# Copies for sums in DRAM, spread behind the weight loads, and six plain chunks at the head of the FFN

## The chip, the cores and the metric

The kernel runs on one NeuronCore of a Trainium2 chip. The metric is the device time of one launch in microseconds: 1307.48 us for the kernel before (median of two runs, 1306.55 and 1308.41). A core has five engines that run side by side, each with its own in-order queue: TensorE (PE, matmuls into PSUM), VectorE (DVE), ScalarE (ACT), GpSimd (POOL), and SyncE (SP), which here only issues DMAs. Sixteen DMA engines move the data for all of them.

## The reference

Two layers of a decoder trunk over 512 tokens of width 1024, in float32. Each layer normalises its input, multiplies it with one wide input weight, runs four groups of heads on parts of the result (attention with a forget gate "f", gated linear attention "g", latent attention "m", and a state-space scan "s"), multiplies their joint output with `w_out`, adds that to the residual, and runs a gated FFN:

```python
for l in range(DEPTH):
    h = rmsnorm(x, norm1[l])
    (fq, fk, fv, ff, gq, ...) = split_cols(h @ w_in[l], IN_SPLITS)
    ...
    x = x + mix @ w_out[l]
    h2 = rmsnorm(x, norm2[l])
    x = x + (silu(h2 @ w_gate[l]) * (h2 @ w_up[l])) @ w_down[l]
return rmsnorm(x, final_norm)
```

The FFN is 2816 wide, 22 chunks of 128 columns.

## The kernel before

All activations stay in SBUF, transposed (features on partitions, 512 tokens along the row). Every weight is cut on the host into units of 128 x 1024 floats (512 KB), in the order in which they are used. Float32 precision is reached with three matmuls per product: weight and activation are each split into a high and a low part, and `prod` (L425) multiplies high by high, low by high and high by low. So each unit is loaded by SP (L314, tile "wr", two buffers), split by ScalarE (the high part "wh", L331) and VectorE (the low part "wl", L332, three buffers each) and then read by 24 matmuls.

A layer takes 34 units ahead of its FFN: two for the first columns, "sm" for the small ones, eight for the convolution and gate columns ("ft"), then "fk", "fq", "fv", "fk", "fq", "mckv", "mcq", "gq", "gk", "gv" and the rest, and eight for `w_out`. Between these products the four groups run as generators, a step at a time. POOL takes part in them: it fills "fkb" and "fqb" (L1227, L1228), multiplies "ce" (L752) and "ssm_mix" (L774) for the scan "s", whose products on TensorE are called "y" (L766, L770), and "gmn" (L797), and clears "gat" (L881) for "g".

The FFN runs in three parts of 8, 8 and 6 chunks of hidden columns; each part ends with eight units of `w_down` ("d"). The first `PLAIN` chunks of the first part are plain: a unit of `w_gate` ("g") and one of `w_up` ("u"), 24 matmuls of 512 columns each. The others go in pairs of chunks: the two chunks and the two halves of the tokens and features form 2 x 2 blocks, multiplied with seven products of half size in place of eight (`pair_products`, L489). A pair has 14 such products, each 12 matmuls of 256 columns. It needs sums of blocks of the activation, which the class `Halves` makes on ScalarE and VectorE, one `chunk(k)` (L467) for each of four feature chunks k, behind plain chunk k. And it needs sums of quadrants of the weights. Those are made in two ways. A pair unit (a gate or an up weight) takes three units of the weight array. `pair_load` (L370) brings two tiles of it to SBUF, "px" and "pz", half of each from the weights and half from a tensor "sum" in DRAM, and "pv"; `pairs` adds two more sums on VectorE (L416, L417), and `pair_part` splits each into high and low ("pX", "pY", "pZ", "pV").

The tensors "sum" are made by `background` (L388), a step of which is called for every unit that is split. SP copies a unit of the weights within DRAM to a new "sum" (L399), and later POOL issues a DMA that adds another unit to it (L395). That POOL instruction waits until its copy has landed. The list `todo` holds the pair units of both layers, 36; a step is taken from the sixth call on, at each call while more than 18 are left, then at every second.

Outside the few stretches under a manual schedule, a scheduler sets the order of the instructions on each engine; it is free to move an instruction that depends on nothing, as a copy within DRAM, ahead of others that come earlier in the code. `tc.issue_after(ins)` is a bound on it: the instructions of the block on the engine of `ins` stand behind `ins` in its queue. It adds no wait on the chip.

Of the kernel before, what the change touches and what calls it, by code (L numbers as in the profile page):

```python
# [52 lines left out]
ACT_SET = "natural_log_exp_and_others"  # L53
HID_PARTS = ((0, 8), (8, 16), (16, 22))

PLAIN = 4
HALF = KC // 2
PAIR_AHEAD = 3
EARLY = 3
# [12 lines left out]
def _weights(I, depth=2):  # L72
# [3 lines left out]
    def add(*ws):  # L76
        u = np.concatenate([_unit(w) for w in ws], 1)
        shapes.append((u.shape[1] // ws[0].shape[1], ws[0].shape[1]))
        units.append(np.pad(u, ((0, 0), (0, 1024 - u.shape[1]))))

    for l in range(depth):
# [25 lines left out]
        for j0, j1 in HID_PARTS:  # L107
            for j in range(j0, min(j1, PLAIN)):
                add(I["w_gate"][l][:, j * P:j * P + P])
                add(I["w_up"][l][:, j * P:j * P + P])  # L110

            paired[len(units)] = (j1 - max(j0, PLAIN)) // 2, not j0
            for j in range(max(j0, PLAIN), j1, 2):

# [35 lines left out]
def trunk(tc, I, out, shapes, paired, depth=2):  # L150
    nc = tc.nc
    PE, V, S, G = nc.tensor, nc.vector, nc.scalar, nc.gpsimd

    def blk(i, n=P):
        return slice(i * n, (i + 1) * n)

    from contextlib import ExitStack
    with ExitStack() as es:
# [14 lines left out]
        def ps_proj(name):  # L173
            return pj.tile([P, T], F32, tag="pj", name=name)

        def ps_mix(name):
            return pm.tile([P, T], F32, tag="pm", name=name)
# [13 lines left out]
        def tmp(tag, name, cols=T, dt=F32, parts=P):  # L191
            return mp.tile([parts, cols], dt, tag=tag, bufs=RINGS[tag], name=name)
# [107 lines left out]
        class Weights:  # L300
# [7 lines left out]
            def load(self, parts=1):  # L308
                i, (nk, ncol) = self.n, shapes[self.n]
                self.n += 1  # L310
                raw = wp.tile([P, 1024], F32, tag="wr", bufs=RAWS, name=f"wr{i}")
                self.loaded.append((raw, i, nk, ncol))
                for c in (blk(j, nk * ncol // parts) for j in range(parts)):
                    nc.sync.dma_start(raw[:, c], I["weights"][i][:, c])  # L314
                    yield

            def split(self, pieces=1):

                if not self.loaded:
                    list(self.load())  # L320

                    if self.n + EARLY in paired and not paired[self.n + EARLY][1]:
                        n, self.n = self.n, self.n + EARLY
                        self.early = self.pair_load(True)
                        self.early_n, self.n = self.n, n
                self.background()
                raw, i, nk, ncol = self.loaded.pop(0)
                n = nk * ncol
                h, lo = (wp.tile([P, 1024], F32R, tag=f"w{c}", bufs=PARTS, name=f"w{c}{i}") for c in "hl")
                for c in (blk(j, n // pieces) for j in range(pieces)):  # L330
                    S.copy(h[:, c], raw[:, c])  # L331
                    V.tensor_tensor(lo[:, c], raw[:, c], h.bitcast(F32)[:, c], op=ALU.subtract)  # L332
                    yield h, lo
                self.ready.append(tuple(t[:, :n].rearrange("p (k c) -> p k c", k=nk) for t in (h, lo)))

            def prefetch(self, n):
# [51 lines left out]
            def background(self):  # L388

                self.turn += 1  # L390
                if self.turn < 6 or self.turn % 2 and len(self.todo) <= 18:
                    return
                if len(self.copied) > (3 if self.todo else 0):
                    i, t = self.copied.pop(0)
                    nc.gpsimd.dma_start(t, I["weights"][i + 2], accum_op=ALU.add, max_dma_last_dim=4096)  # L395
                if self.todo:
                    i = self.todo.pop(0)
                    t = self.sums[i] = dp.tile([P, 1024], F32, name=f"sum{i}")
                    nc.sync.dma_start(t, I["weights"][i + 1])  # L399
                    self.copied.append((i, t))  # L400
# [26 lines left out]
        def prod(ps, w, act, c0=0, ks=None, t=slice(0, T), nk=None, between=lambda: None):  # L427

            wh, wl = w
            n = len(act) if ks is None else nk or KC  # L430
            for k in range(n) if ks is None else ks:
                ah, al = (a[:, t] for a in act[k])
                PE.matmul(ps, lhsT=wh[:, k, c0:c0 + P], rhs=ah, start=k == 0, stop=False)  # L433
                between()
                PE.matmul(ps, lhsT=wl[:, k, c0:c0 + P], rhs=ah, start=False, stop=False)  # L435
                between()
                last = PE.matmul(ps, lhsT=wh[:, k, c0:c0 + P], rhs=al, start=False, stop=k == n - 1)  # L437
            return last
# [692 lines left out]
        for l in range(depth):  # L1131
# [14 lines left out]
            for j in range(10):  # L1146
# [11 lines left out]
                else:  # L1158
                    c = tmp("f", f"cv{l}_{j}")
# [165 lines left out]
            for j0, j1 in HID_PARTS:  # L1325
                us = []
                for j in range(j0, min(j1, PLAIN)):
                    pg, pu = ps_proj(f"g{l}_{j}"), ps_mix(f"u{l}_{j}")
                    if r is None:
                        r = norm2.first_two(pg, pu, KC - 2, with_col=False)  # L1330
                    else:
                        prod(pg, W.get(), act)
                    t, s = tmp("f", f"ft{l}_{j}"), tmp("f", f"fs{l}_{j}")
                    V.tensor_tensor(t, pg, r, op=ALU.mult)
                    silu = S.activation(s, t, AF.Silu)
                    G.tensor_tensor(s, s, r, op=ALU.mult)
                    if j:
                        prod(pu, W.get(), act)
                    V.tensor_tensor(t, pu, s, op=ALU.mult)
                    uh, ul = tmp("a", f"uh{l}_{j}", dt=F32R), tmp("b", f"ul{l}_{j}", dt=F32R)  # L1340
                    S.copy(uh, t)
                    V.tensor_tensor(ul, t, uh.bitcast(F32), op=ALU.subtract)
                    us.append((uh, ul))
                    if j == 0:
                        quads = Halves(l, 16 + l * 8, r)
                    quads.chunk(j)
                lo, hi = slice(0, 256), slice(256, 512)
                for j in range(max(j0, PLAIN), j1, 2):
                    s1, s2, end = pair_products(f"g{l}_{j}", quads.act)
                    S.activation(s1, s1, AF.Silu)  # L1350
                    S.activation(s2[:, hi], s2[:, hi], AF.Silu, scale=-1.0)
                    silu = S.activation(s2[:, lo], end, AF.Silu, scale=-1.0)
                    t1, t2, end = pair_products(f"u{l}_{j}", quads.act)
                    V.tensor_tensor(t1, t1, s1, op=ALU.mult)
                    V.scalar_tensor_tensor(t2[:, hi], t2[:, hi], -1.0, s2[:, hi], op0=ALU.mult, op1=ALU.mult)
                    V.scalar_tensor_tensor(t2[:, lo], end, -1.0, s2[:, lo], op0=ALU.mult, op1=ALU.mult)
                    for i, t in enumerate((t1, t2)):
                        uh, ul = tmp("a", f"uh{l}_{j + i}", dt=F32R), tmp("b", f"ul{l}_{j + i}", dt=F32R)
                        S.copy(uh, t)
                        V.tensor_tensor(ul, t, uh.bitcast(F32), op=ALU.subtract)  # L1360
                        us.append((uh, ul))
                if j1 == HC:
                    with tc.issue_after(silu.ins):
                        S.preload_act_table_set(ACT_SET)
                if j1 == HC and last_layer:
                    last_part(us)
                    continue
                for m in range(KC):
                    ps = ps_proj(f"d{l}_{j0}_{m}")
                    prod(ps, W.get(), us)  # L1370
                    V.tensor_tensor(xT[m], xT[m], ps, op=ALU.add)  # L1371
                    if j1 == HC:
                        norm.chunk(m)
                        norm.square(m)
# [25 lines left out]
```

## Time and profile before

| | us |
|---|---|
| runs shown: median of 2 (lowest, highest) | 1307.48 (1306.55, 1308.41) |
| profiled execution, its time | 1306.41 |
| its span, first to last instruction | 1304.7 |
| TensorE busy (7702 matmuls) | 1220.3 (94%) |
| VectorE busy | 862.6 (66%) |
| ScalarE busy | 652.5 (50%) |
| POOL busy | 132.9 (10%) |
| DRAM copies and accumulates | 36 and 36, 512 KB each |

The chain that ended last is 67% TensorE, 9% DMA, 9% issue and 8% VectorE. Busy shares are means over stages that differ: a share of 94% says nothing of a stage in which TensorE stands still. Matmuls overlap, so that one lasts 389 ns in the records while the next starts after some 230; durations of a row of matmuls are read from start to start. The granted clock of TensorE is 1.00 or 0.50 at a time (2.4 or 1.2 GHz), and a figure between is a mean over a stretch.

### The profile page before, as it was taken

What the parts mean: (1) busy time and instruction counts of PE and PEld (TensorE: products, weight loads), DVE (VectorE), ACT (ScalarE), POOL (GpSimd) and SP (SyncE); (2) the same over time, 40 slices, a digit from 0 to 9 for tenths busy, and PEclk for the clock granted to TensorE, in tenths of its full rate; (3) what the DMA queues carried; (4) which work ended last, traced back from release to release, by engine and by line L of the source; (5) the groups of instructions that cost most, each with busy time, mean ns of one, the idle gap of its engine ahead of it and who ended that gap; (6) DMA issues with size and microseconds to landing.
All of it is one profiled execution on the core that took longest, in us unless ns stands there. A gap on an engine that the chain in (4) does not pass through costs nothing.

```text
span 1304.7 us, 19729 instructions
## 1 busy us (share of the span) xinstructions
PE 1220.3 (94%) x7702; PEld 1058.7 (81%) x7702; DVE 862.6 (66%) x1476; ACT 652.5 (50%) x1126; POOL 132.9 (10%) x151
## 2 busy tenths in 40 slices
PE   8887089999979999999999999999997999999997
PEld 7766068777869899989988887877887989988986
DVE  6654158976887367637755767985888537854764
ACT  5334167574655145515553468857555425533542
POOL 1221243010010000000030012210010000000001
PEclk9989589999989999999999999999998999999999
DMA  9999971122245234423233221121234424341322
GB/s 279 314 298 305 257 155 58 49 66 64 78 149 170 88 110 133 134 73 112 63 105 97 94 84 51 42 69 61 66 114 163 131 84 140 114 142 61 114 62 77
DMA packets 54814, 157.42 MB, mean 121 GB/s; under 512 B 6976, under 2 KB 7136, under 8 KB 54144
## 3 DMA queue, kind: packets, MB, share of 16 engines
q1 hardware_dynamic: 48528, 136.60, 31.6%
q0 software_dynamic: 5760, 18.96, 7.7%
q8 instruction: 60, 0.98, 0.3%
q10 hardware_dynamic: 432, 0.60, 0.2%
q14 instruction: 34, 0.28, 0.1%
HBM read 153.97 MB, written 39.85 MB: 149 GB/s over the span
## 4 chain that ended last, share of the span: by engine, by line
PE 67%; DMA 9%; issue 9%; DVE 8%; ACT 4%; POOL 2%; SPq 0%; DVEq 0%; POOLq 0%; ACTq 0%
PE d L437 5%; PE d L435 5%; PE d L433 5%; DMA sum<-in_weights_dram 4%; DMA wr<-in_weights_dram 4%; PE ft L433 2%; PE ft L437 1%; PE ft L435 1%; DVE wl L332 1%; PE oa L433 1%; PE dl L433 1%; PE dl L437 1%; PE dl L435 1%; PE oa L437 1%; PE sm L918 1%
## 5 line engine op out<-in xcount | busy, mean ns | idle before, releaser
L331 ACT CAST wh<-wr 128x1024 fp32r<-128x1024 f32 (+2 forms) x134 | 134.4, 1004 | 255.9 <-PE d L437 87.8
L332 DVE TENSOR_TENSOR wl<-wr,wh 128x1024 fp32r<-128x1024 f32 (+2 forms) x134 | 156.5, 1168 | 88.0 <-ACT wh L331 87.6
L433 PE MATMUL d<-uh,wh 128*128 128x512 f32 x304 | 118.3, 389 | 0.0
L435 PE MATMUL d<-uh,wl 128*128 128x512 f32 x304 | 118.3, 389 | 0.0
L437 PE MATMUL d<-ul,wh 128*128 128x512 f32 x304 | 118.3, 389 | 0.0
L1371 DVE TENSOR_TENSOR xT<-xT,d 128x512 f32<-128x512 f32 x40 | 27.5, 688 | 98.7 <-PE d L437 98.7
L437 PEld LDWEIGHTS d<-ul,wh 128*128 128x128 f32 x304 | 57.1, 188 | 11.8
L435 PEld LDWEIGHTS d<-uh,wl 128*128 128x128 f32 x304 | 57.1, 188 | 11.7
L433 PEld LDWEIGHTS d<-uh,wh 128*128 128x128 f32 x304 | 57.1, 188 | 11.7
L395 POOL DMA_DIRECT2D sum<-in_weights_dram x36 | 30.4, 868 | 114.1 <-DMA sum<-in_weights_dram 114.1
L586 POOL TENSOR_TENSOR n_1acc<-n_1acc,n_1q 128x512 f32<-128x512 f32 x6 | 9.7, 1614 | 299.1 <-ACT n_1q L585 296.8
L433 PE MATMUL ft<-n_0h,wh 128*128 128x512 f32 x80 | 33.9, 424 | 6.4 <-ACT fo L1166 3.5
L1007 POOL TENSOR_TENSOR nfacc<-nfacc,nfq 128x512 f32<-128x512 f32 x5 | 8.0, 1610 | 297.4 <-ACT nfq L1003 297.4
L435 PE MATMUL ft<-n_0h,wl 128*128 128x512 f32 x80 | 33.0, 412 | 0.1
L437 PE MATMUL ft<-n_0h,wh 128*128 128x512 f32 x80 | 32.9, 411 | 0.0
L770 PE MATMUL y<-ce,st 128*64 128x128 f32 x48 | 6.6, 312 | 26.7 <-POOL ce L752 26.7
L435 PE MATMUL ft<-n_1h,wl 128*128 128x512 f32 x80 | 31.3, 391 | 0.0
L433 PE MATMUL ft<-n_1h,wh 128*128 128x512 f32 x80 | 31.3, 391 | 0.0
L437 PE MATMUL ft<-n_1h,wh 128*128 128x512 f32 x80 | 31.2, 390 | 0.0
L1166 ACT ACTIVATE fo<-fa 128x512 f32<-128x512 f32 x20 | 12.4, 629 | 31.5 <-DVE fa L1164 28.3
L1164 DVE SCALAR_TENSOR_TENSOR fa<-cv,pcv,fa 128x511 f32<-128x511 f32 (+2 forms) x36 | 26.9, 748 | 0.7
L770 PEld LDWEIGHTS y<-ce,st 128*64 128x64 f32 x48 | 4.6, 158 | 27.5 <-POOL ce L752 27.5
(2618 smaller groups left out, 4237.1 us busy)
## 6 DMA issues: line engine op xcount, KB each, us to landing
wr<-in_weights_dram SPq DMA_DIRECT2D x112, 512.0 KB, 3.5
sum<-in_weights_dram SPq DMA_DIRECT2D x36, 512.0 KB, 14.8
sum<-in_weights_dram POOLq DMA_DIRECT2D x36, 512.0 KB, 24.3
px<-in_weights_dram SPq DMA_DIRECT2D x36, 256.0 KB, 4.3
px<-sum SPq DMA_DIRECT2D x36, 256.0 KB, 4.7
pz<-sum SPq DMA_DIRECT2D x36, 256.0 KB, 2.8
pz<-in_weights_dram SPq DMA_DIRECT2D x36, 256.0 KB, 3.2
pv<-in_weights_dram SPq DMA_DIRECT2D x36, 256.0 KB, 3.5
```

The source lines that it names most:

```text
L331: S.copy(h[:, c], raw[:, c])
L332: V.tensor_tensor(lo[:, c], raw[:, c], h.bitcast(F32)[:, c], op=ALU.subtract)
L395: nc.gpsimd.dma_start(t, I["weights"][i + 2], accum_op=ALU.add, max_dma_last_dim=4096)
L433: PE.matmul(ps, lhsT=wh[:, k, c0:c0 + P], rhs=ah, start=k == 0, stop=False)
L435: PE.matmul(ps, lhsT=wl[:, k, c0:c0 + P], rhs=ah, start=False, stop=False)
L437: last = PE.matmul(ps, lhsT=wh[:, k, c0:c0 + P], rhs=al, start=False, stop=k == n - 1)
L586: (adds or (V if k == KC - 1 else G)).tensor_tensor(self.acc, self.acc, sq, op=ALU.add)
L770: PE.matmul(y[blk(hh, 64), blk(b)], lhsT=sv[b - 1][:, blk(2 * g + hh, 64)], rhs=ces[hh][:, blk(b - 1)], start=False, stop=True)
L918: PE.matmul(ps[:, :n], lhsT=q[:d, blk(qb)], rhs=k[:d, :n], start=i == 0, stop=i == len(terms[h]) - 1)
L1164: V.scalar_tensor_tensor(a[:, n:], c[:, :T - n], wc(3 - n), a[:, n:], op0=ALU.mult, op1=ALU.add)
L1166: silu = S.activation(o, a, AF.Silu)
L1371: V.tensor_tensor(xT[m], xT[m], ps, op=ALU.add)
```

## The change

`background` is called behind the split of a unit instead of ahead of it, inside `tc.issue_after` of the last weight load that was traced. It acts at every second call from the sixth on, whatever is left. An accumulate follows when more than one copy is outstanding, where it was more than three. `PLAIN` is 6 instead of 4, so that the first part of each FFN has six plain chunks and one pair (four plain and two pairs before), and `todo` holds 32 pair units. `Halves.chunk` still runs four times, behind the first four plain chunks.

```diff
-PLAIN = 4
+PLAIN = 6
 HALF = KC // 2
...
             def load(self, parts=1):
...
-                    nc.sync.dma_start(raw[:, c], I["weights"][i][:, c])
+                    self.last_load = nc.sync.dma_start(raw[:, c], I["weights"][i][:, c])
                     yield
...
             def split(self, pieces=1):
...
-                self.background()
                 raw, i, nk, ncol = self.loaded.pop(0)
...
                     yield h, lo
+                with tc.issue_after(self.last_load.ins):
+                    self.background()
...
             def background(self):
                 self.turn += 1
-                if self.turn < 6 or self.turn % 2 and len(self.todo) <= 18:
+                if self.turn < 6 or self.turn % 2:
                     return
-                if len(self.copied) > (3 if self.todo else 0):
+                if len(self.copied) > (1 if self.todo else 0):
...
-                    quads.chunk(j)
+                    if j < HALF:
+                        quads.chunk(j)
```

The order of the instructions moves at three places. The first is SP's queue after the load of the input; "wr" is the load of a weight unit, "sum" a copy within DRAM. Before:

```order
L198 DMA xT_92<-in_x_dram 128x512
L314 DMA wr_241<-in_weights_dram 128x1024
L314 DMA wr_311<-in_weights_dram 128x1024
L399 DMA sum_401<-in_weights_dram 16x8192
L399 DMA sum_452<-in_weights_dram 16x8192
L314 DMA wr_317<-in_weights_dram 128x1024
L399 DMA sum_506<-in_weights_dram 16x8192
L399 DMA sum_548<-in_weights_dram 16x8192
L314 DMA wr_399<-in_weights_dram 128x1024
```

Now:

```order
L198 DMA xT_92<-in_x_dram 128x512
L314 DMA wr_241<-in_weights_dram 128x1024
L314 DMA wr_311<-in_weights_dram 128x1024
L314 DMA wr_317<-in_weights_dram 128x1024
L314 DMA wr_399<-in_weights_dram 128x1024
L400 DMA sum_405<-in_weights_dram 16x8192
L314 DMA wr_450<-in_weights_dram 128x1024
L314 DMA wr_502<-in_weights_dram 128x1024
L400 DMA sum_508<-in_weights_dram 16x8192
```

Before, all 36 copies of the program stand ahead of the 21st load of a weight; now a copy stands behind every second load, 21 of 32 ahead of the first pair of layer 0 and the other 11 among the loads of that layer's `w_down`.

The second place is POOL's queue around the scan of layer 0. Before:

```order
L1228 DMA fqb_0_887<-jrr_441 2x512
L1228 DMA fqb_1_896<-jrr_441 2x512
L395 DMA sum_3772<-in_weights_dram 128x1024
L395 DMA sum_3837<-in_weights_dram 128x1024
L395 DMA sum_3913<-in_weights_dram 128x1024
L752 TENSOR_TENSOR ce_0_1003<-ce_0_1003,fo_8_714 128x384
L395 DMA sum_3980<-in_weights_dram 128x1024
L395 DMA sum_5052<-in_weights_dram 128x1024
```

Now:

```order
L1229 DMA fqb_1_883<-jrr_441 2x512
L753 TENSOR_TENSOR ce_0_987<-ce_0_987,fo_8_707 128x384
L396 DMA sum_1069<-in_weights_dram 128x1024
L753 TENSOR_TENSOR ce_1_1051<-ce_1_1051,fo_8_707 128x384
L1228 MEMSET fkb_2_1097 4x512
L1229 DMA fkb_2_1097<-jrr_441 2x512
L396 DMA sum_1267<-in_weights_dram 128x1024
L1228 MEMSET fkb_3_1106 4x512
L775 TENSOR_TENSOR ssm_0mix<-ssm_0mix,fo_2_433 128x512
```

Before, 31 accumulates stand ahead of the first "ce" and 35 ahead of the second; now 6 and 7.

The third place is VectorE's queue at the last chunk of `Halves` in layer 0 ("xn", "bn", "bd" and the low parts "bsl", "b21l", "bd1l", "bd3l"). Before:

```order
L416 TENSOR_TENSOR px_3198<-px_3198 128x512
L1339 TENSOR_TENSOR ft_3_3241<-u_3_3197,fs_3_3242 128x512
L417 TENSOR_TENSOR px_3198<-px_3198,pz_3199 128x512
L472 SCALAR_TENSOR_TENSOR xn_3_3285<-xT_88,pcv,n_0r 128x512
L1342 TENSOR_TENSOR ul_3_3282<-ft_3_3241,uh_3_3281 128x512
L369 TENSOR_TENSOR pY42l<-px_3198,pY42h 128x1024
L369 TENSOR_TENSOR pZ42l<-pz_3199,pZ42h 128x1024
L472 SCALAR_TENSOR_TENSOR xn_7_3287<-xT_92,pcv,n_0r 128x512
```

Now:

```order
L331 TENSOR_TENSOR wl_3211<-wr_3208,wh_3210 128x1024
L1340 TENSOR_TENSOR ft_3_3203<-u_3_3172,fs_3_3204 128x512
L331 TENSOR_TENSOR wl_3275<-wr_3272,wh_3274 128x1024
L1343 TENSOR_TENSOR ul_3_3243<-ft_3_3203,uh_3_3242 128x512
L473 SCALAR_TENSOR_TENSOR xn_3_3246<-xT_88,pcv,n_0r 128x512
L473 SCALAR_TENSOR_TENSOR xn_7_3248<-xT_92,pcv,n_0r 128x512
```

The sums and splits of the first pair's weights stood between the operations of the last chunk; now the splits of two more plain units stand there, and the pair's come behind the chunk.

## Rows read from the trace of the kernel before

**Rows 1.** The profile's 40 slices: busy tenths, granted clock and DMA share in tenths.
```profile
PE   8887089999979999999999999999997999999997
...
PEclk9989589999989999999999999999998999999999
DMA  9999971122245234423233221121234424341322
```
**Rows 2.** Windows "sm" to "mckv", both layers: length, busy (records) by engine, PEclk, DMA, GB/s.
```profile
19.60:179.10 159.50, 105.01 (x512) 86.55 (x511) 72.76 (x139) 52.05 (x86) 40.90 (x55) 0.83 1.04 283
693.60:787.30 93.70, 93.41 (x506) 78.82 (x506) 65.84 (x122) 49.81 (x81) 11.76 (x18) 1.00 0.29 91
```
**Rows 3.** Waits of PE, 0 to 180 us: us in total, times, longest.
```profile
PE y L770 <- POOL ce L752: 26.7, 2, 22.6
PE y L766 <- DVE sw L759: 11.8, 1, 11.8
```
**Rows 4.** Waits of POOL and ACT, 0 to 185 us.
```profile
POOL sum L395 <- DMA sum<-in_weights_dram: 114.1, 31, 16.2
ACT wh L331 <- DMA wr<-in_weights_dram: 61.5, 14, 8.6
```
**Rows 5.** DMA, 0 to 200 us: queues (packets, MB, engines' share); weight loads, median landing.
```profile
q0 software_dynamic: 5504, 18.93, 50.1%
q1 hardware_dynamic: 5953, 33.24, 44.2%
...
wr<-in_weights_dram SPq DMA_DIRECT2D x22, 512.0 KB, 10.7
```
**Rows 6.** Line 399, the copies: ns of issue, first and last start; landing.
```profile
L399 SPq DMA_DIRECT2D sum<-in_weights_dram x36: 488/587/867, 12.9 to 122.0; - x36
...
DMA to landing us min/median/max: 6.0/14.8/21.0
```
**Rows 7.** DMA, 655 to 860 us: weight loads of layer 1, median landing.
```profile
wr<-in_weights_dram SPq DMA_DIRECT2D x29, 512.0 KB, 3.5
```
**Rows 8.** Timelines of layer 1 (start, duration): a load, its cast, the second "ce".
```profile
714.64 0.33 SPq L314 DMA_DIRECT2D wr<-in_weights_dram  x1
...
723.56 1.06 ACT L331 CAST wh<-wr 128x1024 fp32r<-128x1024 f32 x1
...
772.72 1.03 POOL L752 TENSOR_TENSOR ce<-ce,fo 128x384 f32<-128x384 f32 x1 [4.84 <-ACT ce L751]
```
**Rows 9.** Waits of PE, 355 to 400 us (960 to 1010 reads the same).
```profile
PE g_4a L444 <- ACT bsh L465: 5.0, 1, 5.0
PE g_4a L446 <- DVE bsl L466: 2.4, 1, 2.4
```
**Rows 10.** Timeline of PE: first matmul of plain units, first pairs, and steady pairs.
```profile
358.95 0.39 PE L433 MATMUL g<-n_0h,wh 128*128 128x512 f32 x1
...
364.39 0.39 PE L433 MATMUL u<-n_0h,wh 128*128 128x512 f32 x1
...
369.83 0.28 PE L444 MATMUL g_4a<-bsh,pX42h 128*128 128x256 f32 x1
...
400.19 0.28 PE L444 MATMUL g_6a<-bsh,pX48h 128*128 128x256 f32 x1
...
484.20 0.28 PE L444 MATMUL g_10a<-bsh,pX68h 128*128 128x256 f32 x1
...
504.36 0.28 PE L444 MATMUL g_12a<-bsh,pX74h 128*128 128x256 f32 x1
...
977.92 0.28 PE L444 MATMUL g_4a<-bsh,pX162h 128*128 128x256 f32 x1
...
1008.21 0.28 PE L444 MATMUL g_6a<-bsh,pX168h 128*128 128x256 f32 x1
```
**Rows 11.** Timeline of DVE: the end of the last Halves chunk, layer 0.
```profile
382.49 0.68 DVE L466 TENSOR_TENSOR bd3l<-bd,bd3h 128x512 fp32r<-128x512 f32 x1
```
**Rows 12.** DMA issues of the page: "px" from the sums, median us to landing.
```profile
px<-sum SPq DMA_DIRECT2D x36, 256.0 KB, 4.7
```

## The prediction, made before the changed kernel was timed

> **What bounds the kernel now.** I read the 40 slices of the profile first [rows 1]. TensorE is busy 8 to 9 tenths nearly everywhere; the exceptions are the first five slices, up to 163 us, one dip at slice 12 and one at slice 31. In those places the granted clock falls too, and over the same first five slices the DMA row stands at 9 and above. So the kernel is bound by TensorE except at its start, and the question is what the start would cost without its disturbance.
>
> The trace answers that by itself, because layer 1 runs the same program. I take the stretch from the first product of "sm" to the first product of "mckv" in both layers [rows 2]. It holds the same work, 512 and 506 matmul records. Layer 1 needs 93.70 us, with TensorE busy for 93.41 of them at full clock and a DMA share of 0.29. Layer 0 needs 159.50 us at a clock of 0.83 and a DMA share of 1.04. The excess is 65.8 us: 159.50 - 105.01 = 54.5 us idle, and 105.01 - 93.41 = 11.6 us more busy time for the same matmuls, which I put down to the lower of the two clock levels.
>
> Who is waited for [rows 3]: TensorE loses 26.7 us to POOL's "ce" and 11.8 to "sw". Behind them stand the rows of the whole core [rows 4]: POOL itself waits 114.1 us for copies of "sum" to land, with "ce" behind it in its queue, and ScalarE waits 61.5 us for weights, with everything else of ScalarE behind that wait. What fills the DMA engines is in [rows 5]: in the first 200 us the accumulates (q0) take 50.1% and SP's queue (q1) 44.2%. All 36 copies are issued between 12.9 and 122.0 us and land after a median of 14.8 us [rows 6]. Weight loads land after 10.7 us there, and after 3.5 us in layer 1 [rows 5, 7].
>
> The other two dips are the head of the FFN. In layer 0 TensorE waits 5.0 + 2.4 us for the high and low part of the last Halves chunk [rows 9]; layer 1 has two such waits. The first pair takes 400.19 - 369.83 = 30.36 us, in layer 1 1008.21 - 977.92 = 30.29, against 504.36 - 484.20 = 20.16 for a steady pair [rows 10]. The loss is 10.20 and 10.13 us, clock included. VectorE is the cause: it ends that chunk only at 382.49 + 0.68 = 383.2 us [rows 11], 13 us after the plain products are through.
>
> **The change, part by part.**
>
> Copies. There are 32 instead of 36 (two pair units fewer in each layer), and their place on the queues changes far more than the diff suggests: before, all 36 stand on SP ahead of the 21st weight load; now one stands behind every second load, 21 of them ahead of the first pair, 11 in layer 0's down products. On POOL 31 accumulates stood ahead of the first "ce" and 35 ahead of the second; now 6 and 7. Demand of the DMA engines [rows 5]: 50.1% of 200 us over 36 accumulates is 2.8 us each; 44.2% of 200 us over 33.24 MB is 1.4 us for 0.52 MB, be it a copy or a weight unit. Before, 36 copies in 109 us need 36 x (2.8 + 1.4) = 151 us without any weights, more than there is. Now two units of weights bring one copy and one accumulate: 3 x 1.4 + 2.8 = 7.0 us in the 2 x 5.44 = 10.9 us that TensorE takes for two units [rows 10], a load of 0.64. The queue no longer grows, so the term is layer 1's duration: **-65.8 us**.
>
> What stays of it. The low bound is nothing, layer 1 itself. For the high bound: from accumulate 7 on, about seven still stand on POOL ahead of work that TensorE needs ("ce", "ssm_mix", "gmn", "gat"), each waiting for its own copy, which takes 6.0 us at the least [rows 6]: 7 x 6.0 = 42 us if POOL had no slack. It has: it idles 4.84 us before the second "ce" of layer 1 [rows 8]. A weight load has 723.56 - 714.64 = 8.9 us before its cast needs it [rows 8], so 3.5 us may grow to 8.9 at no cost. The stage is nearer to the layer 1 rows than to saturation, so I keep 5 us: **+5**.
>
> FFN head. Per layer one pair becomes two plain chunks. A plain unit takes 364.39 - 358.95 = 5.44 us [rows 10]; four are 21.76, against 20.16 for a pair: +1.60. The two extra chunks bring no Halves chunk (those stay at four), so VectorE has 21.8 us of products in which to finish. The order shows it: the parts of the first pair, which stood ahead of the last chunk, go behind it, and two weight splits take their place. The first pair then starts with its operands ready, if its own loads are in time; "px" from the sums lands after 4.7 us [rows 12], and its slots come free with the last plain splits, one unit (5.4 us) before. So -10.20 + 1.60 = -8.60 and -10.13 + 1.60 = -8.53, together **-17.1**, and I hold back 1 us for a late load: **+1**. The bounds are -17.1 and +3.2 (gap unchanged, extra products paid).
>
> Copies in layer 0's down products, 11: the same load of 0.64, where TensorE does not wait today; nothing, covered by the same 8.9 us. Were that gone, each could cost the accumulate's 2.8 us, 31 us in all.
>
> Sum: the profiled execution took 1306.41 us (span 1304.7), so 1306.4 - 65.8 + 5 - 17.1 + 1 = 1229.5. The median of the runs shown, 1307.48, lies 1.1 above it. I predict **1230 us**.
>
> **The rule against it.** The rows show that copies issued early hold up both the weights and POOL [rows 4, 6]. The Trainium skill, "DMA: Bandwidth & Descriptors", section "Rules for kernel authors", advises the opposite order for overlap: issue the DMA early and wait late. By that rule moving the copies back gains nothing at the start and the sum is the third rival's 1290. The same page of the skill, section "Issuing engines are not separate DMA queues", says that DMAs of SP and of GpSimd run on the same 16 engines and interleave; the trace agrees, with 50.1% and 44.2% side by side.
>
> **The rivals.**
> 1. *POOL's queue takes over.* Each accumulate still stops POOL until its copy has landed, and POOL's products are on TensorE's path. For it: "y" waited for "ce" and nothing else of that size. Against: 6 instead of 31 stand ahead of the first "ce", and single ones between the later steps. Price: seven waits of 6.0 us less 9 us of slack, 33 us kept: 1306.4 - 65.8 + 33 - 16 = 1258.
> 2. *The FFN gap stays*, because the first pair's raw tiles are weight buffers and its loads now stand behind four more weight loads. For it: 4.7 us of landing against 5.4 of cover is thin. Against: those loads do not wait for VectorE's chunk any more. Price: 1230 + 20.3 = 1250.
> 3. *The start is slow for layer 0's own work* (rope tables, constants, selectors), and early copies were harmless. For it: VectorE is busy 72.76 us there, 65.84 in layer 1 [rows 2]. Against: that is 7 us, and POOL's 114.1 us name the copies. Price: only the FFN gain, 1306.4 - 16.1 = 1290. This is where the rule above would lead.
> 4. *Slower: the weight loads starve for the whole of layer 0.* A load behind a copy and its accumulate lands as late as copies do, 14.8 us, past its cover of 8.9 us, 32 times: 1306.4 - 82.9 + 32 x 5.9 = 1412. It decides when loads land later than about 12.1 us in the mean ((76.9 + 26) / 32 = 3.2 us past the cover). Against: even under saturation the median was 10.7.
>
> **How the numbers follow.** The forecast has 0.68, the rivals 0.16, 0.08, 0.05 and 0.03. The forecast's own cases run from 1223 (nothing held back) to about 1238; the range goes down to 1221 for what the rows cannot resolve and up to 1258, which takes in rival 2 and the milder half of rival 1, and leaves out less than 2 in 10. About 2% is what a measurement here tells from no change, 26 us: the forecast and rivals 1 and 2 are faster, 0.92; rival 3 is no change, 0.05; rival 4 is slower, 0.03.
>
> **What would show it.** Right: the stretch from "sm" to "mckv" in layer 0 takes 94 to 101 us at a clock near 1.0, weight loads land in 4 to 8 us, copies are spread up to about 600 us, POOL's wait for them falls from 114 us to under 30, and the first pair takes 20 to 21 us in both layers. Wrong: waits of TensorE for "ce", "ssm_mix" or "sn" of several us (rival 1), "px" or "pX" ahead of the first pair (rival 2), a DMA share of 1 through layer 0 (rival 4).

## The result, and the profile after

The changed kernel takes 1225.54 us (median of two runs, 1225.16 and 1225.91) against 1307.48: a ratio of 0.937, 95% interval 0.933 to 0.941. The prediction was 1230 us, range 1221 to 1258. The profiled execution took 1225.91 us with a span of 1224.0, 80.7 us shorter than before.

The slices of the page (busy tenths, granted clock, DMA share) answer to [rows 1]:

```profile
PE   9999999999999999999999999999999999999997
...
PEclk9999999999999999999999999999999999999999
DMA  6766444456885346532523221112326333432222
```

TensorE is now busy throughout, at the high clock level, and no slice of the DMA row is at 9. The DMA work that filled the first five slices lies spread over the first half. The first windows below answer to [rows 2]: "sm" to "mckv" in layer 0, then in layer 1 (length, busy and records of PE, PEld, DVE, ACT, POOL, then clock, DMA share, GB/s).

```profile
19.21:115.26 96.05, 94.33 (x512) 79.70 (x511) 73.03 (x139) 52.54 (x85) 18.22 (x27) 1.00 0.67 180
622.13:715.84 93.71, 93.43 (x505) 78.83 (x505) 65.81 (x122) 49.78 (x81) 11.70 (x18) 1.00 0.29 91
```

Layer 0's stretch fell from 159.50 to 96.05 us, layer 1's stayed. VectorE's 73 us of work there did not change, so layer 0's own extra work was not what cost the time. The DMA share is 0.67 where it was 1.04, and the prediction's demand sum was 0.64. The DMA view of 0 to 200 us answers to [rows 5] (queue, packets, MB, engines' share; then issues, count, KB each, median us to landing):

```profile
q1 hardware_dynamic: 6176, 24.38, 35.3%
q0 software_dynamic: 2192, 6.87, 21.6%
...
wr<-in_weights_dram SPq DMA_DIRECT2D x28, 512.0 KB, 3.7
sum<-in_weights_dram SPq DMA_DIRECT2D x13, 512.0 KB, 5.3
sum<-in_weights_dram POOLq DMA_DIRECT2D x13, 512.0 KB, 6.1
```

Weight loads land after 3.7 us instead of 10.7, which is layer 1's 3.5 [rows 7] nearly. Thirteen accumulates run there instead of 36. The copies themselves (one line's instructions, first and last start; landing) answer to [rows 6]:

```profile
L400 SPq DMA_DIRECT2D sum<-in_weights_dram x32: 494/498/599, 22.6 to 584.4; - x32
...
DMA to landing us min/median/max: 4.3/5.1/7.3
```

The waits of the whole core, 0 to 185 us, answer to [rows 4]:

```profile
POOL sum L396 <- DMA sum<-in_weights_dram: 107.6, 10, 25.5
...
ACT wh L330 <- DMA wr<-in_weights_dram: 5.7, 4, 3.0
```

ScalarE's wait for weights fell from 61.5 us to 5.7. POOL's wait for copies did not fall: 107.6 us against 114.1, in 10 waits instead of 31. What is left of TensorE's waits, 0 to 180 us, answers to [rows 3]:

```profile
PE sn L537 <- ACT sn_0h L529: 1.5, 1, 1.5
PE pps L221 <- DVE ones L212: 1.1, 1, 1.1
...
PE sn L537 <- DVE sn_0l L530: 0.2, 1, 0.2
```

"ce" and "sw" are gone from it. Around both heads of the FFN (255 to 350 and 900 to 1224 us) the view of TensorE's waits has no row of the pairs, where [rows 9] had 7.4 us a layer. The first pair takes 20.3 us in both layers, against 30.36 and 30.29 [rows 10], with TensorE busy for all of it; "px" from the sums lands as before [rows 12]:

```profile
px<-sum SPq DMA_DIRECT2D x32, 256.0 KB, 4.6
```

Measured from one first matmul to the next, the difference of the two traces is made of these pieces:

| piece | before | after | difference |
|---|---|---|---|
| "sm" to "mckv", layer 0 | 159.49 | 96.06 | -63.43 |
| FFN head to first "d", layer 0 | 94.83 | 86.20 | -8.63 |
| FFN head to first "d", layer 1 | 94.75 | 86.20 | -8.55 |
| first eight units of "d", layer 0 | 43.55 | 44.81 | +1.26 |
| ahead of "sm", and the tail | 67.08 | 66.09 | -0.99 |
| all else | | | -0.32 |
| span | 1304.71 | 1224.05 | -80.66 |

### The profile page after: what moved, and what is told of

Read it like the earlier page. It is cut to its first block, busy times and chain, and to the rows that moved or that the text cites. A ratio compares the mean times of both kernels' runs of the same rounds, so it can differ in the third digit from the quotient of the medians.

```text
span 1224.0 us, 19340 instructions
## 1 busy us (share of the span) xinstructions
PE 1207.7 (99%) x7558; PEld 1043.7 (85%) x7558; DVE 847.6 (69%) x1450; ACT 642.5 (52%) x1104; POOL 140.7 (11%) x151
## 4 chain that ended last, share of the span: by engine, by line
PE 85%; DVE 5%; ACT 5%; issue 2%; DMA 2%; POOL 1%; SPq 0%; DVEq 0%; POOLq 0%; ACTq 0%
PE d L438 6%; PE d L436 5%; PE d L434 5%; PE ft L436 3%; PE ft L434 3%; PE ft L438 3%; PE g L434 2%; PE g L438 2%; PE u L434 2%; PE u L438 2%; PE g L436 2%; PE u L436 2%; PE sm L919 2%; PE oa L434 1%; PE oa L438 1%
## 5 line engine op out<-in xcount | busy, mean ns | idle before, releaser
L330 ACT CAST wh<-wr 128x1024 fp32r<-128x1024 f32 (+2 forms) x142 | 142.7, 1006 | 205.9 <-PE d L438 92.4
L331 DVE TENSOR_TENSOR wl<-wr,wh 128x1024 fp32r<-128x1024 f32 (+2 forms) x142 | 166.0, 1170 | 45.9 <-ACT wh L330 45.0
L1373 DVE TENSOR_TENSOR xT<-xT,d 128x512 f32<-128x512 f32 x40 | 27.5, 687 | 97.5 <-PE d L438 97.5
L396 POOL DMA_DIRECT2D sum<-in_weights_dram x32 | 26.5, 827 | 439.6 <-DMA sum<-in_weights_dram 439.2
L434 PE MATMUL ft<-n_0h,wh 128*128 128x512 f32 x80 | 31.6, 395 | 0.5 <-ACT wh L330 0.5
L438 PE MATMUL ft<-n_0h,wh 128*128 128x512 f32 x80 | 31.4, 392 | 0.0
L1337 POOL TENSOR_TENSOR fs<-fs,n_1r 128x512 f32<-128x512 f32 x6 | 13.5, 2260 | 101.4 <-ACT fs L1336 101.4
L417 DVE TENSOR_TENSOR px<-px 128x512 f32<-128x512 f32 x32 | 22.1, 691 | 1.0
L418 DVE TENSOR_TENSOR px<-px,pz 128x512 f32<-128x512 f32 x32 | 21.9, 685 | 0.2
```

Of the source, the lines that this page charges most:

```text
L417: V.tensor_tensor(x[:, 512:1024], x[:, 512:1024], x[:, 0:512], op=ALU.add)
L418: V.tensor_tensor(x[:, 0:512], x[:, 512:1024], z[:, 512:1024], op=ALU.add)
```

## The experiments

The theory to test, D: in layer 0's start the DMA engines held more than they could move, so weights came late. Its rivals: P, POOL's queue alone (its waits ahead of "ce"); R, the order on SP's queue (loads stand behind copies). For the FFN: V, VectorE's volume of work ahead of the first pair; L, the first pair's own loads. In each row the ratio is to the kernel before, run on the same chip.

| kernel | us | ratio, 95% interval | "sm" to "mckv", layer 0 |
|---|---|---|---|
| the change's copies alone | 1241.35 | 0.948, 0.947 to 0.950 | 97.5 |
| six plain chunks alone | 1281.15 | 0.978, 0.977 to 0.980 | 152.3 |
| change without the bound | 1280.78 | 0.978, 0.976 to 0.980 | 154.3 |
| a copy behind every load | 1225.74 | 0.936, 0.935 to 0.937 | 96.5 |
| before, no accumulates | 1240.98 | 0.948, 0.947 to 0.950 | 94.3 |
| before, POOL free | 1284.73 | 0.982, 0.980 to 0.983 | 139.8 |
| before, second transfer plain | 1279.61 | 0.977, 0.976 to 0.979 | 133.6 |
| change, no sums at all | 1222.43 | 0.934, 0.933 to 0.936 | 94.2 |
| copies alone, three Halves chunks | 1233.74 | 0.943, 0.941 to 0.944 | 94.8 |
| copies alone, two Halves chunks | 1220.7 | 0.933, 0.932 to 0.934 | 95.6 |
| copies alone, differences on POOL | 1245.63 | 0.952, 0.951 to 0.954 | 95.7 |
| change, ssm_mix on VectorE | 1221.3 | 0.933, 0.932 to 0.935 | 93.9 |

**The two halves of the change.** The change with four plain chunks, and the kernel before with six:

```diff
-PLAIN = 6
+PLAIN = 4
```

> The copies moved as in the change, but four plain chunks as before. Theory that the two parts add up: the start of layer 0 gains its 63.4 us, the head of the FFN keeps its gap, 1307.5 - 63.6 = 1244 us; first pair again 30 us in both layers. Rival, that the parts need each other (the late sums would hold up the first pair when it comes two chunks earlier): above 1250.

```diff
-PLAIN = 4
+PLAIN = 6
...
-                    quads.chunk(j)
+                    if j < HALF:
+                        quads.chunk(j)
```

> Six plain chunks, copies as before. Theory that the parts add up: only the gap at the head of the FFN goes, 1307.5 - 17.2 = 1290 us, the stretch sm to mckv stays at about 159 us (four copies and accumulates fewer could take up to 10 us off it). Rival, that the gap closes only when nothing else disturbs the loads: 1300 or more.

Measured: 1241.35 and 1281.15 us. In the first, the start is repaired and the pairs' gap stays (50.9 us from the first pair to "d", as before); in the second, the pairs take 20.3 us and the start still 152.3. The second also has four copies and accumulates fewer, which took 7 us off the start. Otherwise the halves nearly add up, but for one thing that neither does alone: the first eight units of "d" in layer 0 take 43.55 us in both kernels and 44.81 in the change.

**The place or the rate.** The change without `issue_after`:

```diff
-                with tc.issue_after(self.last_load.ins):
-                    self.background()
+                self.background()
```

> The changed kernel without the bound that puts a copy behind the last load; a copy is still traced for every second unit. The scheduler then puts all 32 copies ahead of the 20th load. Theory that the place on the queue is what counts: the start is lost again, 1275 to 1290 us. Rival, that the lower rate and the later call are enough: 1226 us.

Measured 1280.78 us. The copies are asked for at every second unit, but nothing holds them there: the view of their line reads as in the kernel before.

```profile
L399 SPq DMA_DIRECT2D sum<-in_weights_dram x32: 488/587/963, 11.8 to 113.6; - x32
...
DMA to landing us min/median/max: 5.9/14.6/21.3
```

So the start stays at 154.3 us. What counts is the bound behind the loads; asking for the copies less often does nothing by itself, since the kernel takes the same time as the six plain chunks alone.

**Twice the rate, with the bound.**

```diff
-                if self.turn < 6 or self.turn % 2:
+                if self.turn < 6:
```

> The changed kernel with a copy behind every load in place of every second. By the demand 2 x 1.4 + 2.8 = 5.6 us of all DMA engines per 5.4 us of matmuls. Theory D (the DMA engines are overcommitted): the queue grows slowly, weight loads land after 6 to 10 us, the start loses 5 to 25 us, 1230 to 1250 us. Theory P (accumulates ahead of POOL's products): 12 and 13 accumulates stand ahead of the two ce products in place of 6 and 7, but each waits for its own copy alone, 1226 to 1231 us.

Measured 1225.74 us, no slower than the change; that is under D's 1230 to 1250 and just under P's range. The window "sm" to "mckv" of this kernel and its copies' line:

```profile
19.60:116.10 96.50, 94.40 (x513) 79.77 (x511) 72.91 (x139) 53.17 (x86) 22.38 (x31) 1.00 0.92 258
```

```profile
L400 SPq DMA_DIRECT2D sum<-in_weights_dram x32: 494/495/1057, 22.9 to 255.5; - x32
...
DMA to landing us min/median/max: 4.3/6.7/9.2
```

At a DMA share of 0.92 weight loads land after a median of 5.4 us, within the 8.9 us that a load has [rows 8]. TensorE stands for 2.1 us, in one wait for "sn", behind two accumulates that stand on POOL ahead of "ssm_mix" (the change has one there and waits 1.7 us):

```profile
PE sn L537 <- ACT sn_0h L529: 2.1, 1, 2.1
```

My demand sum called this rate more than the engines have (5.6 us of transfers for 5.4 us of products); it was too high by a tenth, and theory D with it. The step to harm lies between this share and the 1.04 of before; the plain transfers below narrow it.

**Which of the transfers.** The kernel before without its 36 accumulates (sums are then only copies), with its copies still hoisted to the head:

```diff
                     i, t = self.copied.pop(0)
-                    nc.gpsimd.dma_start(t, I["weights"][i + 2], accum_op=ALU.add, max_dma_last_dim=4096)
```

> The kernel before with its 36 early copies but without the 36 accumulates (they are left out, so the sums are only copies). Theory D: the demand falls to (36 + 20) x 1.4 = 78 us in 109, the DMA engines keep up, 1243 to 1255 us. Theory P: POOL waits for nothing any more, also about 1244. Rival R (weight loads stand behind two to five copies in SP's own queue, whatever the load): loads still land late, 1265 us or more.

Measured 1240.98 us: the whole gain of the start, and 94.3 us for the stretch. Its window:

```profile
19.24:113.54 94.30, 94.16 (x512) 79.69 (x511) 73.28 (x139) 52.10 (x85) 11.72 (x18) 1.00 0.80 284
```

The order on SP, with all 36 copies issued from 12.6 to 92.5 us as before among the first weight loads, cost nothing once the accumulates were gone. So R falls. D and P both allow this, since an accumulate loads the engines and stops POOL; the next kernel parts them: the one before with everything that others wait for taken off POOL, the accumulates left there.

```diff
-                    G.tensor_tensor(ce, ce, Cm[g][:, P:T], op=ALU.mult)
+                    V.tensor_tensor(ce, ce, Cm[g][:, P:T], op=ALU.mult)
...
-                G.tensor_tensor(t, t, z[g], op=ALU.mult)
+                V.tensor_tensor(t, t, z[g], op=ALU.mult)
...
-                        G.memset(b.bitcast(F32)[64:68], one)
-                        nc.gpsimd.dma_start(b[row:row + 2], rr[h:h + 65:64])
+                        V.memset(b.bitcast(F32)[64:68], one)
+                        nc.scalar.dma_start(b.bitcast(F32)[row:row + 2], rr.bitcast(F32)[h:h + 65:64])
```

> The kernel before with nothing of the scan or of the attention behind the accumulates: ce and ssm_mix are multiplied on VectorE, fkb and fqb cleared on VectorE and filled by ScalarE's DMA queue. Theory P: the 38.5 us of waits at y and the clock lost there come back, 1245 to 1260 us. Theory D: the weights still land after 10 us and the first 20 units are not there before 120 us, 1275 to 1300 us.

Measured 1284.73 us, D's number. Two rows of its waits, 0 to 185 us:

```profile
POOL sum L395 <- DMA sum<-in_weights_dram: 135.8, 36, 15.2
ACT wh L331 <- DMA wr<-in_weights_dram: 59.0, 14, 8.6
```

ScalarE's wait for weights is nearly what it was (61.5 us, [rows 4]), and no wait of TensorE up to 185 us names POOL any more. Of the start's 65.8 us, POOL's queue is worth 159.5 - 139.8 = 19.7 while the weights are late; 46 us stay. That these belong to the late weights is read from the waits and not measured by itself: this kernel also gives VectorE 5.7 us more work in the stretch (78.5 against 72.8) and ScalarE's queue eight DMAs.

**The adding or the volume.** The kernel before, its accumulates turned into plain transfers of the same bytes by the same queue:

```diff
-                    nc.gpsimd.dma_start(t, I["weights"][i + 2], accum_op=ALU.add, max_dma_last_dim=4096)
+                    nc.gpsimd.dma_start(t, I["weights"][i + 2], max_dma_last_dim=4096)
```

> The kernel before, with its 36 accumulates turned into plain transfers of the same 512 KB by the same queue at the same places (they overwrite the copy, so the sums are not sums). Every queue keeps its order and its waits. Theory A (it is the adding that loads the DMA engines: an accumulate took 2.78 us of all 16 engines in the kernel before, 50.1% of 200 us over 36, and a copy some 1.4 us where there were no accumulates): 36 transfers of 1.4 us take 50 us off the 16 engines in the first 180 us, the weight loads land in 4 to 6 us, and most of the start's 64 us come back: 1241 to 1260. Theory B (two transfers per unit from two queues are too many there, adding or not): the stretch from sm to mckv stays over 140 us and the time over 1285.

Measured 1279.61 us, which neither theory met. Its DMA view, 0 to 200 us, and its window "sm" to "mckv":

```profile
q1 hardware_dynamic: 6421, 34.69, 47.9%
q0 software_dynamic: 5504, 18.93, 28.0%
```

```profile
19.22:152.79 133.57, 102.61 (x512) 85.28 (x511) 72.89 (x139) 52.37 (x86) 30.17 (x54) 0.87 0.96 343
```

The adding is a true cost: 28.0% of 200 us over 36 is 1.56 us of all engines for a plain transfer, against 2.78 with the add, and the stretch gains 25.9 us. But the engines stay all but full, at 343 instead of 283 GB/s [rows 2], and weight loads still land after 9.1 us. So both the adding and the volume at the head count; of these kernels, only those without accumulates or with spread ones have loads that land in time. The windows from 19 to 80 us show the step (the kernel before, this one, and a copy behind every load):

```profile
19.00:80.00 61.00, 51.30 (x222) 40.83 (x221) 36.77 (x79) 20.52 (x28) 14.04 (x17) 0.95 1.03 300
19.00:80.00 61.00, 55.64 (x242) 44.66 (x241) 39.85 (x83) 21.96 (x29) 8.79 (x17) 0.94 1.00 358
19.00:80.00 61.00, 61.00 (x286) 50.13 (x285) 50.32 (x97) 30.58 (x42) 8.23 (x10) 1.00 0.94 276
```

At a DMA share of 0.94 TensorE is busy all the time, with 286 matmul records; at 1.00 there are 242, at 1.03 222. No wait of TensorE in these windows names POOL, so what is lost in them is lost without POOL's queue.

**What the spread sums still cost.** The change without copies and accumulates (pairs read an unsummed unit):

```diff
-                with tc.issue_after(self.last_load.ins):
-                    self.background()
...
-                i, wt, sums = self.n, I["weights"], self.sums.pop(self.n)
+                i, wt = self.n, I["weights"]
+                sums = wt[i + 1]
```

> The changed kernel with no copies and no accumulates at all (the pairs read an unsummed unit in place of the sums). It shows what the spread copies still cost: the start of layer 0 should fall from 96.1 to the 93.7 us of layer 1 and the first down products from 44.8 to 43.6 us, 1222 us. Theory that the moved copies cost nothing: 1225.5. Theory that they still delay loads all through layer 0: below 1218.

Measured 1222.43 us, 3.1 below the change. Its trace differs in two places: 94.2 instead of 96.1 us in the start, and 43.55 instead of 44.81 for the first "d". The first has its reason on POOL. The timeline of POOL in the changed kernel (start, duration, instruction, idle before it and what ended that):

```profile
108.85 0.88 POOL L396 DMA_DIRECT2D sum<-in_weights_dram  x1 [7.54 <-DMA sum<-in_weights_dram]
109.43 0.52 POOL L1228 MEMSET fkb<- 4x512 f32 x1
110.04 1.29 POOL L775 TENSOR_TENSOR ssm_0mix<-ssm_0mix,fo 128x512 f32<-128x512 f32 x1
```

VectorE hands ssm_0mix over at 106.88 + 0.75 = 107.63 us, but POOL stands at an accumulate, waiting for its copy, and "sn" follows late. Five kernels of this study run the same program up to there, and differ in when that copy lands:

| accumulate issued, us | TensorE's waits for "sn", us | "sm" to "mckv", us | kernel |
|---|---|---|---|
| 107.47 | 0.4 | 94.8 | three Halves chunks |
| 108.35 | 1.2 | 95.6 | two Halves chunks |
| 108.66 | 1.3 | 95.7 | differences on POOL |
| 108.85 | 1.7 | 96.1 | the change |
| 108.99 | 1.9 | 97.5 | copies alone |

A later landing, a longer wait. The copies alone lose 1.3 us more than their wait: behind it the clock fell (a mean of 0.79 from 110 to 117 us, 1.00 in the change). The second place is on ScalarE:

```profile
349.66 1.05 ACT L330 CAST wh<-wr 128x1024 fp32r<-128x1024 f32 x1 [5.05 <-DMA wr<-in_weights_dram]
350.61 0.61 ACT L1361 CAST uh<-u 128x512 fp32r<-128x512 f32 x1
```

The third unit of "d" is late (6.4 us from the issue of its load to its cast, 4.0 without the sums), at a DMA share of 0.98 in the stretch of the pair, and the pair's own high part "uh" stands behind its cast; without the sums that cast starts 0.6 us ahead of the first "d" (345.24 against 345.82), here 1.9 us behind it. In the kernel with a copy behind every load, whose last copy is issued at 255.5 us, the same eight units take 43.55. So they do in the copies alone, where no accumulate is issued between 322.0 and 362.7 us; the change issues one at 337.4, 5.8 us ahead of that load. That this accumulate is what delays the load is not tested.

**The first place, tested**: ssm_mix on VectorE in the changed kernel.

```diff
-                G.tensor_tensor(t, t, z[g], op=ALU.mult)
+                V.tensor_tensor(t, t, z[g], op=ALU.mult)
```

> The kernel as changed, with the multiplication of ssm_mix on VectorE instead of POOL (0.7 us, twice a layer). Theory M (the 2.4 us that the start of layer 0 kept is the wait of ssm_0mix behind the accumulate that waits on POOL for its copy): that start falls from 96.1 us to 93.7 to 94.5, in all 1223 to 1224. Rival N (what is kept is the loaded DMA engines, or VectorE's 0.7 us cost as much as the wait): no change, 1225 to 1226.

Measured 1221.3 us (1220.69 to 1221.49), 4.2 below the change and the lowest of the kernels here that compute all. Its window:

```profile
18.82:112.68 93.86, 93.86 (x512) 79.78 (x511) 73.70 (x140) 52.53 (x85) 16.42 (x25) 1.00 0.68 181
```

TensorE never stands in that stretch, at the same DMA load, though the accumulate is issued as late as in the change (108.71 us). So M holds for most of the 2.2 us that the stretch gives, out of the 4.6 by which the span is shorter. Some 0.4 of the 2.2 need no accumulate: layer 1's start, beside which none runs, gains as much (93.71 to 93.30), and VectorE makes the product in 0.68 us where POOL took 1.29. The other 2.4 are small shifts (0.6 in each layer between "mckv" and `w_out`, 0.5 in the first "d", those 0.4 in layer 1 and 0.4 ahead of "sm") that I did not trace. The two kernels were timed apart, each beside the kernel before, and by the ratios their intervals overlap (0.932 to 0.935 and 0.933 to 0.941).

**The FFN's gap.** The copies alone, with the fourth Halves chunk left out, then with the third and fourth left out:

```diff
             def chunk(self, k):
+                if k == HALF - 1:
+                    for parts in self.act.values():
+                        parts.append(parts[-1])
+                    return
```

> Four plain chunks, copies moved, and the fourth Halves chunk left out (the third one's tiles are read again in its place). Theory V (VectorE is late with that chunk): the gap at the first pair goes in both layers, e1 less 20 us, 1224 us. Theory L (the first pair's own loads are late): the gap stays at 5 us or more per layer, 1234 to 1244 us.

```diff
-                if k == HALF - 1:
+                if k >= HALF - 2:
```

> The copies as changed, four plain chunks, and of the class Halves only the first two chunks made: the third and fourth reuse the parts of the second, so the pairs multiply other data than the reference asks for. Theory V (VectorE's work on the four chunks, some 5.6 us each, is what the first pair waits for): without two of them the pairs' stretch falls from 50.9 us to the 2 x 20.3 that two undisturbed pairs take, 10.2 us less in each layer than the kernel with the copies alone (1241.4), so 1221. Theory L (after one chunk is gone, the first pair's own loads and splits of weights are what it waits for, whatever VectorE has to do): no more than the kernel without the fourth chunk, 1234.

Measured 1233.74 and 1220.7 us. One chunk gave back only 3.6 of the 10.2 us a layer; TensorE then waited for the weights' part "pY" in place of "bsh", and its row is

```profile
PE g_4a L445 <- ACT pY42h L369: 3.2, 1, 3.2
```

That looks like L. But "pY" waits for a sum "px" that VectorE makes, behind the third chunk. Two chunks less close the gap wholly, with the code of the loads as it was: 40.47 us for two pairs and TensorE busy all of it:

```profile
305.26:345.73 40.47, 40.47 (x338) 40.37 (x336) 30.91 (x44) 22.61 (x38) 0.83 (x1) 1.00 0.71 229
```

So V: it is VectorE's backlog. In the copies-alone kernel VectorE is busy without a break in one window of the head and close to it in the next (length, VectorE busy and records, clock, DMA share, GB/s):

```profile
285.00:296.00 11.00, 11.00 (x21) 1.00 0.70 186
296.00:307.40 11.40, 10.21 (x19) 1.00 0.45 154
```

A chunk left out takes work from ScalarE too, but ScalarE is busy for only 5.86 and 5.58 us of these windows. The 1.19 us in which VectorE stands still in the second are a wait for a product of POOL ("fs").

Moving part of VectorE's work to POOL was the attempt to keep four plain chunks:

```diff
-                V.tensor_tensor(n[:, lo], b11, b12, op=ALU.subtract)
+                G.tensor_tensor(n[:, lo], b11, b12, op=ALU.subtract)
...
-                V.tensor_tensor(d[:, lo], b22, b12, op=ALU.subtract)
+                G.tensor_tensor(d[:, lo], b22, b12, op=ALU.subtract)
```

> The copies as changed, four plain chunks, and in each chunk of Halves the two plain differences (b11 - b12 and b22 - b12) on POOL instead of VectorE. Theory V: 2 x 0.42 us leave VectorE in each of four chunks, 3.4 us a layer; leaving out a whole chunk of 5.6 us gave 3.8 us a layer, so 3.4 us give 2.3, in all 1241.4 - 4.6 = 1236.8, with 1232 if each us counts in full. Theory L: 1241. Rival, POOL too slow: its multiplications there took 2.3 to 2.9 us beside a busy VectorE, and an accumulate waits in its queue ahead of one of the differences: 1245 or more.

Measured 1245.63 us, slower than the copies alone by 4.3, as the rival had it. TensorE's wait for "bsh" rose from 5.0 to 8.3 us, and POOL's timeline shows a difference that VectorE made in 0.41 us:

```profile
288.95 0.82 POOL L396 DMA_DIRECT2D sum<-in_weights_dram  x1 [1.57 <-DMA sum<-in_weights_dram]
291.48 2.32 POOL L478 TENSOR_TENSOR bn<-xn 128x256 f32<-128x256 f32 x1 [1.71 <-DVE xn L473]
293.76 0.73 POOL L480 TENSOR_TENSOR bd<-xn,xn 128x256 f32<-128x256 f32 x1
```

It takes 0.7 to 2.3 us there, with VectorE busy beside it, and every chunk now crosses from VectorE to POOL and back. The Trainium skill, "Perfetto Trace Analysis", section "Optimizing Scalar/DVE Operations", warns of this exchange: the two engines share a read port of SBUF, so moving work between them might not help. The rows agree as far as they go; they do not part the port from the crossing.

## Why the prediction was right, step by step

**The start, -65.8 kept +5.** Right. The stretch lost 63.4 us and kept 2.4. That layer 1 is the measure of an undisturbed layer 0 holds closely: 94.2 us without sums, 93.86 in the best kernel, 93.71 in layer 1. The +5 was 2.6 too high. What it stands for was named, accumulates on POOL ahead of "ssm_mix": rival 1 in small, one wait of 7.5 us with most of it slack.

**One sub-claim failed: "POOL's wait for them falls from 114 us to under 30".** It is 107.6. The prediction gives no sum for that figure; it reads as if waits of POOL were harm that had to shrink with the start. They need not be: an accumulate stands early in POOL's queue, and its copy is now held behind weight loads, so POOL stands idle for about as long as before. What changed is who stands behind it: 6 accumulates ahead of the first "ce" instead of 31, and of the ten waits one touches the path. A wait is no cost; a wait with needed work behind it is.

**Weight loads "in 4 to 8 us".** 3.7, slightly better than the low end. The cause given, DMA engines that hold more than they move, holds for the main part: freeing POOL alone left ScalarE's wait for weights and 46 us of the excess, and in the first 61 us of the stretch TensorE lost time to late weights without any wait for POOL. In the kernel before POOL's stops and late weights went together, and the prediction, which gave one term to both, did not need to split them. The split is 19.7 us to POOL's queue, measured while the weights were late.

**The rule against the change.** The prediction set the Trainium skill, "DMA: Bandwidth & Descriptors", section "Rules for kernel authors", against the rows: issue early, wait late. By that rule moving the copies back gains nothing at the start; the kernel without the bound, 1280.78 us, and the change, 1225.54, differ in where the copies stand and show that here it gains 55 us. The rule is not wrong for a transfer by itself: 36 early copies without accumulates did no harm (1240.98 us, and 94.3 us for the stretch). It does not cover transfers that fill the engines ahead of more urgent ones.

**The FFN, -17.1 and +1.** Right to a tenth: -8.63 and -8.55 against -8.60 and -8.53. The cause, VectorE's chunk, is shown by the two chunks left out, where four plain chunks and two pairs take 84.6 us, 1.6 less than the change's 86.2, which is the +1.60 of the sum. The +1 for a late load was of the right size by luck: the load it was held back for, the first pair's, is in time, and 1.3 us are lost behind it at the first "d", where the prediction expected nothing.

**Not in the sum:** -1.0 us ahead of "sm" and in the tail; not followed up.

Rivals 2 and 3 fall by the pair's 20.30 us and by VectorE's unchanged 73 us. Rival 1 is down to 1.7 us of waits for "sn". Rival 4 was the other side of D: at 0.92 of the engines the loads still land in 5.4 us, inside their cover, so it was far from deciding.

## What to carry to other kernels

Where two layers run the same program, the quiet one prices the disturbed one: subtract, and look for what only one of them carries. A transfer that depends on nothing can be hoisted by a scheduler to the head of its queue, as here; bind it behind the loads that matter, since asking for it less often does not hold it there. And move work off a backlogged engine only if the other one is as fast under the same load: leaving the work out first tells what the move can give at most.

## What the runs showed of the hardware that was not expected

- An accumulate from DRAM to DRAM takes nearly twice the DMA engines' time of a plain transfer of the same 512 KB: 2.78 us of all 16 against 1.56 by the same queue at the same place, and 3.32 (21.6% of 200 us over 13) where the engines are not full.
- Contention is steep at the end: from 19 to 80 us a DMA share of 0.94 left TensorE busy all the time, with 286 matmul records; at 1.00 there were 242, at 1.03 222.
- A subtraction of 128x256 on POOL took 0.73 to 2.32 us beside a busy VectorE (medians 1.15 and 0.82 for the two kinds), which makes it in 0.41 to 0.42.
